# The last group of an MLP's second product, as seven half-size products instead of one plain product

## The chip, the cores and the metric

The kernel runs on one core of a Trainium2 chip. The core has five engines that run side by side and meet through semaphores: TensorE (PE, matmuls; its weight loads are the row PEld), VectorE (DVE), ScalarE (ACT), GpSimd (POOL) and SyncE (SP). Transfers between the chip's memory and the core's SBUF are issued here by SP and by GpSimd. The metric is the time of one execution on the device in microseconds (us); a smaller one is better.

## The reference

Two layers of a bidirectional encoder, 512 tokens by 1024 features, float32. Layer 0 mixes tokens with a gated delta rule (GDN), layer 1 with gated linear attention (GLA); after each mixer and after each MLP stands a layer norm of the scaled residual sum. The change lies in the MLP and the norms:

```
def _sq_relu_mlp(h, w1, w2):
    a = jax.nn.relu(jnp.matmul(h, w1))
    return jnp.matmul(a * a, w2)

for i in range(DEPTH):
    m = _mixer_gdn(...) if i % 2 == 0 else _mixer_gla(...)
    x = _layernorm(DEEPNORM_ALPHA * x + m, ln1_g[i], ln1_b[i])
    x = _layernorm(DEEPNORM_ALPHA * x + _sq_relu_mlp(x, mlp_w1[i], mlp_w2[i]), ln2_g[i], ln2_b[i])
```

`w1` is 1024 by 4096, `w2` 4096 by 1024.

## The kernel before

**Precision.** Each float32 operand of a matmul is split into two parts, `hi` and `lo` (`split`, L85): ScalarE casts the operand to `hi` (L95), VectorE subtracts `hi` from it (L96). `mm3` (L111) then issues three matmuls for one product of tiles: `hi*hi`, `hi*lo`, `lo*hi`. Tiles that hold parts are called `wh`/`wl`, `w2h`/`w2l`, `ah`/`al`, `xh`/`xl`; a tag with `bufs` buffers is a ring, so a new tile waits until the oldest one in it has been read for the last time.

**The MLP** works in four groups of 1024 of the 4096 features. The first product makes the activations `h` of a group, the second product multiplies them by 1024 rows of `w2` and adds to the residual `xt` (four tiles of 128 tokens, two halves of 512 columns each). Groups 0 to 2 of the second product run in `second` as seven products of half size: `h` is cut into quarters (`a11`, `a12`: tokens 0 to 255, features 0 to 511 and 512 to 1023; `a21`, `a22`: tokens 256 to 511), `w2` into blocks `(0,0)`, `(0,1)`, `(1,0)`, `(1,1)` of 512 by 512, and sums and differences of these are multiplied. A block is two tiles `w2r` (`q` = 0, 1) of 128 by 1024; `plus` adds one block to another in place on VectorE (L351). Each of the seven products is 24 matmuls of 512 columns, into two PSUM banks with the tags X, Y or Z, and `add` (L464) adds a bank to the residual. Between the products, `nxt` issues the pieces of the first product of the following group, so that VectorE and ScalarE have time for sums and parts.

**The last group** (`last`) has no following group. It computes the plain product: for each of the four token tiles and each column half, 8 x 3 matmuls of 512 columns (bank `pl`), 192 in all, a tile at a time; after each tile follow its two adds and its layer norm, and then either its four-by-two transposes into the next mixer's input (`xpose`, first MLP) or its store (second MLP). The weights are staged by `wrows` through the ring `wst` and split into whichever rings are free.

**The norm** (`layernorm`) has two forms. With `sums` the mean comes from accumulators of the adds and the squares from ScalarE; without, VectorE takes statistics (L223, L224). Then `(x - mean) * g` (L226), the reciprocal root on ScalarE and VectorE (L186 to L195), and `* rstd + b` (L231). Except for the last tile, the second column half of this final step is a ScalarE multiply (L233) and a GpSimd add (L234):

```
for q in range(2):
    if last or q == 0:
        nc.vector.scalar_tensor_tensor(out[q], out[q], rstd[:, 0:1], par[2 + q], ALU.mult, ALU.add)
    else:
        nc.scalar.mul(out[q], out[q], rstd[:, 0:1])
        nc.gpsimd.tensor_tensor(out[q], out[q], par[2 + q], ALU.add)
```

That form runs in the norms after the two mixers; `last` calls with `last=True`.

**Order.** Each engine works through its own list in order. A scheduler sets these lists from the program and from the dependences of the tiles; inside `in_order(engine)` the instructions of that engine keep the order in which they are written.

Of the kernel before, what the change touches and what calls it, by code (L numbers as in the profile page):

```python
# [17 lines left out]
P = 128  # L18
S = 512
# [9 lines left out]
class Ctx:  # L29
# [54 lines left out]

    def split(self, src, shape, pool=None):  # L85

        nc = self.nc
        if pool is None:
            hi = self.whl.tile(shape, F32R, name="wh", tag="wh")
            lo = self.whl.tile(shape, F32R, name="wl", tag="wl")  # L90
        else:
            pool, hi, lo, bufs = pool
            hi = pool.tile(shape, F32R, name=hi, tag=hi, bufs=bufs)
            lo = pool.tile(shape, F32R, name=lo, tag=lo, bufs=bufs)
        nc.scalar.copy(hi, src)  # L95
        nc.vector.tensor_tensor(lo, src, hi.bitcast(F32), ALU.subtract)  # L96
        return hi, lo
# [28 lines left out]

    def proj_halves(self, specs, between=None):


        out = [self.bank([P, S], F32, name=name, tag=tag) for _, name, tag in specs]  # L130
        for hf in range(2):
            sl = slice(hf * 256, hf * 256 + 256)
            for ps, ((wh, wl), _, _) in zip(out, specs):
                n = wh.shape[-1]
                for k in range(KT):
                    if wl is None:
# [70 lines left out]
    def layernorm(self, z, out, par, last=False, sums=None):  # L207
# [21 lines left out]
        for q in range(2):  # L229
            if last or q == 0:  # L230
                nc.vector.scalar_tensor_tensor(out[q], out[q], rstd[:, 0:1], par[2 + q], ALU.mult, ALU.add)  # L231
# [70 lines left out]
def mlp(c, w1, w2, g, b, out=None, extra=None):  # L302
# [14 lines left out]
    with c.banks(pj=2, X=2, Y=2, Z=2), tc.tile_pool(name="mlp", bufs=2) as pool:  # L317
# [20 lines left out]

        def split(i):

            i_, j_ = {1: (0, 0), 2: (1, 0), 3: (1, 1), 4: (1, 0), 5: (0, 0), 6: (0, 0), 7: (0, 1)}[i]
            parts[i] = [c.split(blocks[i_, j_, q], [P, 2, 512], pool=ring("w2")) for q in range(2)]

            sums = {1: ((0, 0), (0, 1)), 2: ((0, 1), (1, 1)), 5: ((0, 0), (1, 1)), 6: ((1, 0), (0, 0))}
            if i in sums:
                plus(*sums[i])

        def plus(a, b):
# [117 lines left out]
        def quarters(h):  # L466
            return [h[j][:, :, HT * i:HT * i + HT] for i in range(2) for j in range(2)]

        def second(gi, h, a, nxt):

            a11, a12, a21, a22 = quarters(h)

            def banks(tag):
                return [c.bank([P, 512], F32, name="p" + tag, tag=tag) for _ in range(2)]

            def product(bk, a, i, new, by_tile=False):

                if i not in parts:
                    split(i)
                ws = parts.pop(i)  # L480
                order = [(q, j) for j in range(2) for q in range(2)] if by_tile else [(q, j) for q in range(2) for j in range(2)]
                for q, j in order:
                    wh, wl = ws[q]
                    sl = slice(j * P, (j + 1) * P)
                    for k in (2 * q, 2 * q + 1):
                        c.mm3(bk[j], a[0][:, k, sl], a[1][:, k, sl], wh[:, k % 2, :], wl[:, k % 2, :],
                              new and k == 0, k == HF - 1, skip_group_check=True)

            def fetch(i, j):
                if gi + 2 < G:  # L490
                    load(gi + 1, i, j)

            X, Y = banks("X"), banks("Y")
            load(gi, 1, 0)
# [3 lines left out]
            nxt()  # L498
            Z = banks("Z")
            product(Z, pair(a12), 2, True)  # L500
# [27 lines left out]
            nxt()  # L528
            if gi + 2 == G:
                nxt()  # L530
                nxt()
# [6 lines left out]

        def last(gi, h):

            par = c.load_ln(g, b, lambda i: pool.tile([P, 512], F32, name="ln", tag=("xh5", "xh6", "xl5", "xl6")[i], bufs=1))
            a, ws = {}, {}

            def part(i, j, home):
                a[i, j] = pair(h[j][:, :, HT * i:HT * i + HT], home)

            def rows(i, home=None):
                ws[i] = c.wrows(w2, (gi * GF + 2 * (i % 4)) * P, i // 4 * 512, pool=ring(home) if home else None)

            rows(0)  # L550
            rows(3, "w2")
            part(0, 0, "ah")
            rows(1)
            rows(2)
            part(0, 1, "raw")
            rows(4, "raw")
            rows(5, "raw")
            rows(6, "w2")
            rows(7, "w2")
            part(1, 0, "ah")  # L560
            part(1, 1, "raw")
            if out is None:
                c.new_x()
            for t in range(NT):
                sl = slice(t % 2 * P, t % 2 * P + P)
                for hf in range(2):
                    ps = c.bank([P, 512], F32, name="pl", tag="YZYZXZXZ"[2 * t + hf])
                    for k in range(GF):
                        wh, wl = ws[4 * hf + k // 2]
                        ah, al = a[t // 2, k // HF]  # L570
                        c.mm3(ps, ah[:, k % HF, sl], al[:, k % HF, sl], wh[:, k % 2, :], wl[:, k % 2, :], k == 0, k == GF - 1)
                    add(t, hf, ps)
                c.layernorm(c.xh(t), c.xh(t), par, last=True)
                if out is None:
                    c.xpose(t, c.xt[t], ("pj",))
                else:
                    nc.sync.dma_start(out[t * P:(t + 1) * P, :], c.xt[t])

# [32 lines left out]
        for gi in range(G - 1):  # L611
            more = gi + 2 < G
            nh = new_h()

            def nxt():
# [16 lines left out]
                step += 1  # L632
                if half == 1 and i % 4 == 2 and more:
                    split(1)
# [50 lines left out]
def gla(c, gc, w_in, gate_w2, w_out, ln_g, ln_b, w_next):  # L685
# [5 lines left out]
    with c.banks(ac=2, tp=2, pj=4), tc.tile_pool(name="gla", bufs=2) as pool:  # L691
# [943 lines left out]
```

## Time and profile before

| | us |
|---|---|
| median of three runs | 1375.24 |
| the three runs | 1370.43, 1375.24, 1376.11 |
| the profiled execution | 1370.78 |
| its span, first to last instruction | 1369.1 |
| last group of the first MLP, first to last matmul `pl` | 721.81 to 770.3 |
| last group of the second MLP, first to last matmul `pl` | 1315.51 to 1360.4 |

The profile is of one execution. A row of the timeline reads: start, duration, engine, line, operation, output<-inputs, shape, count, and in brackets how long the engine idled before it and what ended that. A duration reaches from an instruction's start to its end; instructions of one engine overlap a little, so the time that one occupies is the distance to the next start. In a row of the waits stand the waiting instruction, what it waited for, the total, the number of waits and the longest. In the row of a window stand its length and the busy time of PE, PEld, DVE, ACT and POOL, each with its count, then the granted clock, the DMA share and GB/s. In the chain of waits, followed back from the last instruction, a row is start, length and who held the chain.

### The profile page before, as it was taken

Reading aid. Unit: us, or ns where it says so; the run is one execution under the profiler, and the core shown is the slowest. Engines: PE = TensorE matmul, PEld = TensorE weight load, DVE = VectorE, ACT = ScalarE, POOL = GpSimd, SP = SyncE. Lnnn points to the kernel's source line nnn. Section 1 sums busy time; section 2 is a strip of 40 time slices with the busy share of each in tenths; the row PEclk is TensorE's granted clock in tenths of the full one; section 3 lists DMA queues with packets and bytes.
Section 4 is the critical chain, followed back from the end, with each engine's and each line's share of the span. In section 5 each row is a group of like instructions: output and inputs, shape, how many; then the busy total and the mean of one; then the engine's idle time right before and its main releaser. Section 6 shows DMA issues by size and latency. Waiting matters only on the chain.

```text
span 1369.1 us, 21146 instructions
## 1 busy us (share of the span) xinstructions
PE 1341.5 (98%) x8317; PEld 1123.9 (82%) x8317; DVE 1073.9 (78%) x1685; ACT 738.7 (54%) x1444; POOL 72.5 (5%) x111
## 2 busy tenths in 40 slices
PE   8999999999999999999999999999999999999997
PEld 7777777777777888888887888888878888888886
DVE  7787787778677997897967687977779787979675
ACT  4776668765743655555553354654446455545440
POOL 5000000000003700000000000000000000000000
PEclk9999999999999999999999999999999999999999
DMA  6221112210251523243123332221325153322141
GB/s 190 63 62 48 47 32 63 60 35 32 78 154 57 176 78 108 77 154 93 47 90 100 91 92 76 62 62 62 99 55 185 47 154 92 124 78 60 47 152 49
DMA packets 145222, 117.44 MB, mean 86 GB/s; under 512 B 6571, under 2 KB 121379, under 8 KB 145123
## 3 DMA queue, kind: packets, MB, share of 16 engines
q1 hardware_dynamic: 143779, 111.90, 27.2%
q0 software_dynamic: 1344, 4.20, 1.1%
q8 instruction: 65, 1.06, 0.3%
q14 instruction: 34, 0.28, 0.1%
HBM read 113.99 MB, written 2.10 MB: 85 GB/s over the span
## 4 chain that ended last, share of the span: by engine, by line
PE 83%; ACT 7%; DVE 6%; DMA 2%; issue 1%; POOL 0%; DVEq 0%; SPq 0%; ACTq 0%
PE pj L115 5%; PE pj L116 5%; PE pj L114 5%; PE pX L114 3%; PE pX L115 3%; PE pX L116 3%; PE pjv L114 3%; PE pjv L115 3%; PE pjv L116 3%; PE fxz L114 2%; PE scp L865 2%; PE op L1561 2%; PE fxz L115 2%; PE fxz L116 2%; PE pl L115 2%; PE pl L116 2%
## 5 line engine op out<-in xcount | busy, mean ns | idle before, releaser
L95 ACT CAST wh<-wst 128x1024 fp32r<-128x1024 f32 x146 | 152.8, 1050 | 203.8 <-PE pj L115 49.8
L96 DVE TENSOR_TENSOR wl<-wst,wh 128x1024 fp32r<-128x1024 f32 x146 | 178.9, 1232 | 62.2 <-ACT wh L95 62.1
L115 PE MATMUL pj<-xtl,wh 128*128 128x512 f32 (+1 forms) x352 | 127.1, 361 | 0.5 <-DVE xtl L178 0.5
L114 PE MATMUL pj<-xth,wh 128*128 128x512 f32 (+1 forms) x352 | 126.8, 362 | 0.8 <-ACT xth L177 0.7
L116 PE MATMUL pj<-xth,wl 128*128 128x512 f32 (+1 forms) x352 | 126.7, 361 | 0.0
L96 DVE TENSOR_TENSOR w2l<-w2r,w2h 128x1024 fp32r<-128x1024 f32 x84 | 102.5, 1222 | 26.6 <-ACT w2h L95 26.5
L95 ACT CAST w2h<-w2r 128x1024 fp32r<-128x1024 f32 x84 | 88.2, 1050 | 64.5 <-PE pX L116 28.1
L114 PEld LDWEIGHTS pj<-xth,wh 128*128 128x128 f32 x352 | 66.2, 189 | 11.2 <-ACT xth L177 1.2
L115 PEld LDWEIGHTS pj<-xtl,wh 128*128 128x128 f32 x352 | 66.4, 189 | 10.9 <-DVE xtl L178 0.8
L115 PE MATMUL pX<-w2l,ah 128*128 128x512 f32 x192 | 75.0, 391 | 0.0
L116 PE MATMUL pX<-w2h,al 128*128 128x512 f32 x192 | 74.9, 390 | 0.0
L114 PE MATMUL pX<-w2h,ah 128*128 128x512 f32 x192 | 74.8, 393 | 0.0
L116 PEld LDWEIGHTS pj<-xth,wl 128*128 128x128 f32 x352 | 66.4, 189 | 10.2
L95 ACT CAST ah<-h 128x1024 fp32r<-128x1024 f32 x46 | 48.4, 1053 | 46.8 <-PE pX L115 20.8
L351 DVE TENSOR_TENSOR w2r<-w2r 128x1024 f32<-128x1024 f32 x48 | 58.1, 1233 | 0.3
L96 DVE TENSOR_TENSOR al<-h,ah 128x1024 fp32r<-128x1024 f32 x46 | 56.2, 1221 | 0.6
L114 PE MATMUL pjv<-wh,xth 128*128 128x512 f32 x128 | 54.7, 427 | 0.0
L116 PE MATMUL pjv<-wh,xtl 128*128 128x512 f32 x128 | 50.2, 392 | 0.0
L115 PE MATMUL pjv<-wl,xth 128*128 128x512 f32 x128 | 50.0, 390 | 0.0
L116 PEld LDWEIGHTS pX<-w2h,al 128*128 128x128 f32 x192 | 36.1, 188 | 7.5
L116 PE MATMUL pjk<-xth,wl 128*128 128x512 f32 (+1 forms) x112 | 41.8, 373 | 0.0
L114 PEld LDWEIGHTS pX<-w2h,ah 128*128 128x128 f32 x192 | 35.8, 188 | 7.1 <-ACT w2h L95 0.3
(469 smaller groups left out, 3915.4 us busy)
## 6 DMA issues: line engine op xcount, KB each, us to landing
wst<-in_mlp_w SPq DMA_DIRECT2D x80, 512.0 KB, 4.3
w2r<-in_mlp_w SPq DMA_DIRECT2D x48, 512.0 KB, 3.7
wst<-in_a_w_in SPq DMA_DIRECT2D x32, 512.0 KB, 4.1
wst<-in_b_w_in SPq DMA_DIRECT2D x32, 256.0 KB, 3.0
wst<-in_a_w_out SPq DMA_DIRECT2D x8, 512.0 KB, 3.8
wst<-in_b_w_in SPq DMA_DIRECT2D x8, 512.0 KB, 3.8
wst<-in_b_w_out SPq DMA_DIRECT2D x8, 512.0 KB, 3.6
xt<-in_x SPq DMA_DIRECT2D x4, 512.0 KB, 4.1
```

The source lines that it names most:

```text
L95: nc.scalar.copy(hi, src)
L96: nc.vector.tensor_tensor(lo, src, hi.bitcast(F32), ALU.subtract)
L114: mm(ps, ah, bh, start=start, stop=False, **kw)
L115: mm(ps, ah, bl, start=False, stop=False, **kw)
L116: mm(ps, al, bh, start=False, stop=stop, **kw)
L351: V.tensor_tensor(blocks[a + (q,)], blocks[a + (q,)], blocks[b + (q,)], ALU.add)
L865: T.matmul(ps[:, n, :], kh[:, sl], qh[:, sl], start=True, stop=True)
L1561: T.matmul(op[:, n, :], l, r, start=i == 0, stop=i == len(mm) - 1)
```

## The change

`last` becomes a form of `second` without a following group: seven products of 24 matmuls, 168 instead of 192, in the order 1, 5, 2, 6, 3, 7, 4, into banks X, Y, Z, X, Y, X, X. The products 3, 7 and 4 go tile by tile (`by_tile`), so that a token tile is complete before the product ends. Its blocks of `w2` are loaded ahead as in the other groups.

- The sums of blocks in the last group (`plus` with `by_dma`) are adding transfers that GpSimd issues, SBUF to SBUF, 512 KB each, eight in an MLP.
[...]
- The second part of a block gets homes that have fallen free: the operands' tiles `xh`/`xl`, a tile of `h`, a ring `wh`/`wl`.
- In the last group the lists of GpSimd, ScalarE and VectorE are written out by hand up to product 3, that of PE throughout.
- The accumulating form of `add` (`full`) gives the sums for the norm's first form; all four norms follow product 3. Tiles 0 and 1 are transposed inside product 4, tiles 2 and 3 inside the first projections of the mixer that follows (`at` in `proj_halves`). The output is stored in halves of a tile.
- The norm's final step is always VectorE's: no GpSimd add, no ScalarE multiply.

```diff
-    def split(self, src, shape, pool=None):
+    def split(self, src, shape, pool=None, by_dma=False):
...
         nc.scalar.copy(hi, src)
-        nc.vector.tensor_tensor(lo, src, hi.bitcast(F32), ALU.subtract)
+        if by_dma:
+            nc.scalar.mul(lo, src, -1.0)
+            nc.gpsimd.dma_start(lo, src, accum_op=ALU.add)
+        else:
+            nc.vector.tensor_tensor(lo, src, hi.bitcast(F32), ALU.subtract)
         return hi, lo
...
         for q in range(2):
-            if last or q == 0:
+            if True:
                 nc.vector.scalar_tensor_tensor(out[q], out[q], rstd[:, 0:1], par[2 + q], ALU.mult, ALU.add)
...
+            if homes:
+                for x, y in {1: (((0, 0), (0, 1)), ((0, 1), (1, 1))), 5: (((0, 0), (1, 1)),), 2: (((1, 0), (0, 0)),)}.get(i, ()):
+                    plus(x, y, True)
+                return
...
-                V.tensor_tensor(blocks[a + (q,)], blocks[a + (q,)], blocks[b + (q,)], ALU.add)
+                if by_dma:
+                    nc.gpsimd.dma_start(blocks[a + (q,)], blocks[b + (q,)], accum_op=ALU.add)
+                else:
+                    V.tensor_tensor(blocks[a + (q,)], blocks[a + (q,)], blocks[b + (q,)], ALU.add)
...
             if gi + 2 == G:
+                split(4)
                 nxt()
                 nxt()
...
+        def last(gi, h, a):
...
+            load(gi, 1, 0)
+            X, Y, Z = banks("X"), banks("Y"), banks("Z")
+            split(5, homes[5])
+            V.tensor_tensor(a21, a22, a21, ALU.subtract)
+            a5 = pair(a21)
+            product(X, a, 1, True)
+            a2 = pair(a12)
+            split(2, homes[2])
+            V.scalar_tensor_tensor(a11, a21, -1.0, a11, ALU.mult, ALU.subtract)
+            for j in range(2):
+                add(j, 0, X[j])
+            product(Y, a5, 5, True)
+            a6 = pair(a11)
+            split(6, homes[6])
+            V.scalar_tensor_tensor(a12, a12, -1.0, a11, ALU.mult, ALU.subtract)
+            V.scalar_tensor_tensor(a21, a11, -1.0, a22, ALU.mult, ALU.subtract)
+            for j in range(2):
+                add(2 + j, 1, Y[j], ALU.subtract)
+            product(Z, a2, 2, True)
+            split(7, homes[7])
+            a3 = pair(a12)
+            for j in range(2):
+                full(j, 0, Z[j])
+            split(3, homes[3])
+            product(X, a6, 6, False)
+            t = wide(F32R)
+            split(4, homes[4], (None, t[:, 0:2, :], t[:, 2:4, :], None))
+            a7 = pair(a21)
+            for j in range(2):
+                add(j, 1, X[j], ALU.subtract)
+            product(Y, a3, 3, False, True)
+            orders.close()
+            full(0, 1, Y[0], -1.0)
+            a4 = pair(a22)
+            full(1, 1, Y[1], -1.0)
+            product(X, a7, 7, False, True)
+            norm(0, False)
+            for j in range(2):
+                full(2 + j, 1, X[j], -1.0)
+            norm(1, False)
+            product(X, a4, 4, False, True, turn)
+            for j in range(2):
+                full(2 + j, 0, X[j])
+            return norm
...
-            h, a = nh, nxt.a if more else None
-        last(G - 1, h)
+            h, a = nh, nxt.a
+        with c.in_order(mybir.EngineType.PE):
+            norm = last(G - 1, h, a)
+        norm(2, False)
+        norm(3, True)
...
-        gps, *qk0 = c.proj_halves(specs)
+        with c.in_order(mybir.EngineType.PE):
+            gps, *qk0 = c.proj_halves(specs, at={(0, 2, 4 * j): lambda t=2 + j: c.xpose(t, c.xt[t], ("tp", "pj")) for j in range(2)})
```

How the change moves instructions, at three places. In the rows the line numbers are those of the changed file (L101 is the subtraction of `split`, L479 is `add`, L579 is `full`, L181 a transpose); `xt_5637` to `xt_5640` are the residual tiles 0 to 3.

VectorE in the second MLP's last group, between products 1 and 3:

```order
L101 TENSOR_TENSOR al<-h,ah 128x1024 x2
L101 TENSOR_TENSOR w2l<-w2r,w2h 128x1024
L101 TENSOR_TENSOR xl_13604<-w2r,xh_13603 128x1024
L605 SCALAR_TENSOR_TENSOR h<-h 128x4x256
L479 TENSOR_TENSOR xt_5637<-xt_5637,pX 128x512
L479 TENSOR_TENSOR xt_5638<-xt_5638,pX 128x512
L101 TENSOR_TENSOR al<-h,ah 128x1024
L101 TENSOR_TENSOR w2l<-w2r,w2h 128x1024
L101 TENSOR_TENSOR xl_13645<-w2r,xh_13644 128x1024
L611 SCALAR_TENSOR_TENSOR h<-h 128x4x256
L612 SCALAR_TENSOR_TENSOR h<-h 128x4x256
L479 TENSOR_TENSOR xt_5639<-xt_5639,pY 128x512
```

These are the low parts of the left operands of products 5 and 2, the weights of 2, a difference of quarters, the adds of product 1, and the same again for product 6. Behind them come the second add of product 5, the low part of product 3's left operand, two `full` of product 2, and the low parts of product 3's weights. Before, the last group had only casts, subtractions and `pl` adds without sums of quarters.

VectorE at the end of the second MLP, before:

```order
L464 TENSOR_TENSOR xt_5640<-xt_5640,pl 128x512
L223 BN_STATS bst<-xt_5640 128x6
L224 BN_AGGR bmv<-bst 128x2
L226 SCALAR_TENSOR_TENSOR xt_5640<-xt_5640,bmv,ln 128x512
L188 TENSOR_TENSOR rst<-rsy 128x1
L226 SCALAR_TENSOR_TENSOR xt_5640<-xt_5640,bmv,ln 128x512
L189 SCALAR_TENSOR_TENSOR rst<-bmv,rst 128x1
L190 TENSOR_SCALAR rst<-rst 128x1
L195 TENSOR_TENSOR rstd<-rsy,rst 128x1
L231 SCALAR_TENSOR_TENSOR xt_5640<-xt_5640,rstd,ln 128x512 x2
```

and with the change:

```order
L238 SCALAR_TENSOR_TENSOR xt_5637<-xt_5637,rstd,ln 128x512 x2
L197 TENSOR_SCALAR rst<-rst 128x1
L579 SCALAR_TENSOR_TENSOR xt_5639,lns<-pX,xt_5639 128x512
L202 TENSOR_TENSOR rstd<-rsy,rst 128x1
L224 SCALAR_TENSOR_TENSOR bmv<-lns,bias_83 128x1
L238 SCALAR_TENSOR_TENSOR xt_5638<-xt_5638,rstd,ln 128x512 x2
L579 SCALAR_TENSOR_TENSOR xt_5640,lns<-pX,xt_5640 128x512
L227 SCALAR_TENSOR_TENSOR bmv<-lnq,bias_81 128x1
L233 SCALAR_TENSOR_TENSOR xt_5639<-xt_5639,bmv,ln 128x512
```

The last add of tile 3 (`xt_5640`, L579) now stands behind the ends of the norms of tiles 0 and 1, and what is left of the norm of tile 2 stands between it and the norm of tile 3.

PE at the end of the first MLP, before and with the change:

```order
L116 MATMUL pl<-w2h,w2r 128x512
L174 MATMUL tp<-ident,xt_5639 128x128 x8
L114 MATMUL pl<-w2h,w2r 128x512
L115 MATMUL pl<-w2l,w2r 128x512
L116 MATMUL pl<-w2h,w2r 128x512
```

```order
L121 MATMUL pX<-xh_8568,al 128x512
L181 MATMUL tp<-ident,xt_5637 128x128 x8
L119 MATMUL pX<-h,ah 128x512
L120 MATMUL pX<-h,ah 128x512
L121 MATMUL pX<-h,al 128x512
L119 MATMUL pX<-h,ah 128x512
L120 MATMUL pX<-h,ah 128x512
L121 MATMUL pX<-h,al 128x512
L181 MATMUL tp<-ident,xt_5638 128x128 x8
L119 MATMUL pX<-xh_8568,ah 128x512
```

Before, a tile's transposes stood some 20 matmuls behind its last one; now those of tile 0 stand right behind the first half of product 4, 36 matmuls (product 7's 24 and 12 of product 4) behind the end of product 3, the last product that writes tiles 0 and 1, and those of tile 1 six matmuls later.

More of the change, by code (lines that the diff above doesn't have):

```diff
@@ L498, in second @@
             nxt()
-            Z = banks("Z")
+            Z = banks(tags[1])
             product(Z, pair(a12), 2, True)
@@ L537, in second @@
                 nxt()
[L539 to L561, printed above, removed]
+        def last(gi, h, a):
+            homes = {i: (pool, f"xh{k}", f"xl{k}", 1) for i, k in ((5, 3), (2, 7), (6, 6), (7, 3), (4, 7))}
+            homes[3] = ring("raw")
+            wide = lambda dt: pool.tile([P, HF, S], dt, name="h", tag="h", bufs=3)
+            a11, a12, a21, a22 = quarters(h)
+            sums = [c.small.tile([P, 2], F32, name="lns", tag="lns") for t in range(NT)]
+            par = []
+            for src, tag in ((g, "xh5"), (b, "xl5")):
+                t = pool.tile([P, 2, 512], F32, name="ln", tag=tag, bufs=1)
+                nc.gpsimd.dma_start(t, src.rearrange("(q n) -> q n", q=2).partition_broadcast(P))
+                par += [t[:, 0, :], t[:, 1, :]]
@@ L562, in last @@
             if out is None:
                 c.new_x()
[L564 to L573, printed above, removed]
-                if out is None:
-                    c.xpose(t, c.xt[t], ("pj",))
-                else:
-                    nc.sync.dma_start(out[t * P:(t + 1) * P, :], c.xt[t])
+            ET = mybir.EngineType
```

78 lines of the change are left out of this document (51 added, 27 removed).

## The prediction

> **What bounds the kernel now.** I read the page, then PE's waits, the stages by windows, and last the timelines around the two places where the last group of an MLP runs.
>
> ```profile
> span 1369.1 us, 21146 instructions
> PE 1341.5 (98%) x8317; PEld 1123.9 (82%) x8317; DVE 1073.9 (78%) x1685; ACT 738.7 (54%) x1444; POOL 72.5 (5%) x111
> ...
> PE 83%; ACT 7%; DVE 6%; DMA 2%; issue 1%; POOL 0%; DVEq 0%; SPq 0%; ACTq 0%
> ```
>
> ```profile
> PE tp L174 <- POOL xt L234: 1.4, 3, 0.6
> PE pl L115 <- DVE w2l L96: 1.3, 2, 0.6
> PE pjq L114 <- DVE xt L464: 0.9, 1, 0.9
> ```
>
> PE is busy 98% of the span and its listed waits are small (total, times, longest), so a matmul less is worth its slot. That holds while the other engines keep up; for that I look at VectorE (DVE) by stage: the two norms after the mixers, and the last group of the second MLP (busy us of PE, PEld, DVE, ACT, POOL in turn).
>
> ```profile
> 415.00:440.00 25.00, 22.79 (x127) 17.64 (x127) 23.58 (x52) 9.11 (x20) 7.30 (x8) 1.00 0.00 1
> 1008.00:1036.00 28.00, 24.94 (x149) 20.45 (x149) 24.45 (x58) 12.89 (x30) 4.69 (x3) 1.00 0.03 8
> ...
> 1315.00:1361.00 46.00, 44.81 (x195) 36.02 (x194) 31.02 (x52) 9.62 (x16) 0.00 (x0) 1.00 0.18 68
> ```
>
> VectorE fills 94% and 87% of the norm stages but 67% of the last group. The change adds VectorE work to all three.
>
> **Durations.** Slots are differences of starts in these rows.
>
> ```profile
> 721.81 0.40 PE L114 MATMUL pl<-wh,ah 128*128 128x512 f32 x1
> ...
> 1290.16 0.39 PE L114 MATMUL pY<-w2h,ah 128*128 128x512 f32 x1
> 1290.84 0.39 PE L114 MATMUL pY<-w2h,ah 128*128 128x512 f32 x1
> ...
> 1311.05 0.28 PE L114 MATMUL fxz<-xth,wh 128*128 128x256 f32 x1
> 1311.41 0.40 PE L114 MATMUL pX<-w2h,ah 128*128 128x512 f32 x1
> 1315.51 0.39 PE L114 MATMUL pl<-wh,ah 128*128 128x512 f32 x1
> ...
> 762.84 1.29 PE L174 MATMUL tp<-ident,xt 128*128 128x128 f32 x8
> 763.89 0.48 PE L114 MATMUL pl<-w2h,w2r 128*128 128x512 f32 x1
> 787.58 0.63 PE L779 MATMUL lg<-glr,w2r 96*128 96x512 f32 x2
> ```
>
> Three 512-column matmuls take 0.68 us, so one 0.227 and a half-size product (24) 5.44; three of 256 columns 0.36; eight transposes 1.05. The last group starts at T = 721.81 and T = 1315.51.
>
> ```profile
> 1317.30 1.04 ACT L95 CAST w2r<-wst 128x1024 fp32r<-128x1024 f32 x1
> 1318.25 1.04 ACT L95 CAST ah<-h 128x1024 fp32r<-128x1024 f32 x1
> 1320.30 1.22 DVE L96 TENSOR_TENSOR al<-h,ah 128x1024 fp32r<-128x1024 f32 x1
> 1321.44 1.22 DVE L96 TENSOR_TENSOR w2r<-wst,w2r 128x1024 fp32r<-128x1024 f32 x1
> 1293.95 1.28 DVE L464 TENSOR_TENSOR xt<-xt,pY 128x512 f32<-128x512 f32 x2
> 1009.29 0.68 DVE L292 SCALAR_TENSOR_TENSOR xt<-ob,xt 128x512 f32<-128x512 f32 x1
> 1009.90 0.08 DVE L292 DVE_READ_ACCUMULATOR xt<-ob,xt 128x1 f32 x1
> 1364.13 1.41 DVE L231 SCALAR_TENSOR_TENSOR xt<-xt,rstd,ln 128x512 f32<-128x512 f32 x2
> ```
>
> So a cast costs ScalarE 0.95 (ready after 1.05), a 1024-wide subtraction or sum costs VectorE 1.14 (ready after 1.22), an add from PSUM 0.62, with its accumulator 0.70, a 512-wide norm step 0.67, a 128x1 step 0.1 to 0.2.
>
> **The matmuls.** Each MLP loses 24 of 192: 24 x 0.227 = 5.44, both 10.9. The two waits on w2l (0.6 each) belong to the removed loop. This is the ceiling; three things take from it.
>
> **Inside the last group (second MLP).** In VectorE's order, from the low part of the second product's left operand (its cast needs the first product's slot, free at T+5.6) to the low part of product 3's first weight, stand ten 1024-wide steps, four adds and two accumulating adds: 10 x 1.14 + 4 x 0.62 + 2 x 0.70 = 15.3, from T+6.7 to T+22, ready at T+23.2. Product 3 is the fifth; its second matmul is due at T + 4 x 5.44 + 0.23 = T+22.0. PE waits 1.3. Products 5, 2 and 6 just fit: for 5, sum, cast and low part end 0.3 before its third matmul wants them. ScalarE has 22 casts and multiplies there, 21 us of 38, and its slots never come last: covered. The low parts of products 7 and 4 leave VectorE (4 x 1.14 less) for ScalarE and the adding transfers, and so do eight block sums; I cost both at nothing, and they are hidden behind two to three products each, until a transfer is late (rival C). So five products end at T+28.5, all seven at T+39.4 (1354.9), against the last matmul's end now:
>
> ```profile
> 1360.20 0.24 PE pl L116
> ...
> 1360.46 0.70 DVE xt L464
> ...
> 1364.88 0.66 DVEq L1631
> ```
>
> **The tail (second MLP).** What is late next is VectorE. Before, tiles were finished one by one, with a norm some 11 us apart, and 5.1 us of VectorE followed the last matmul, to 1365.54. Now all four norms stand behind product 3: from the last operand's low part (T+28.5 + 1.05 cast + 1.22 and handovers = T+31.1) VectorE has four accumulating adds (2.8), sixteen norm steps (10.7), two statistics with their merge (1.6) and some 22 small steps (about 3.3): 18.4, done at T+49.5 = 1365.0. PE's 5.4 shrinks to 0.5. The last store is 256 KB instead of 512:
>
> ```profile
> wst<-in_b_w_in SPq DMA_DIRECT2D x32, 256.0 KB, 3.0
> ...
> wst<-in_b_w_in SPq DMA_DIRECT2D x8, 512.0 KB, 3.8
> ```
>
> by these loads 0.8 less. Together **-1.3**; bounds +1 (each handover 0.05 dearer) and -6 (no queue on VectorE).
>
> **The end of the first MLP.** Same walk: norm 0 ends at T+38.1 (no statistics there). Its transposes stand after the first half of product 4, T+36.7: PE waits 1.4. Those of tile 1 need norm 1, which stands behind tile 0's first low part: 0.95 more. Tile 2's need norm 2, 12.5 after norm 0, while PE has 10.5 of work: 1.95. Tile 3 fits. PE's work from T to the end of the projections of q and k is 168 x 0.227 + 4 x 1.05 + 128 x 0.117 = 57.3 (before 62.8 of the 65.8 measured from 721.81 to 787.58); with 1.3 + 1.4 + 0.95 + 1.95 it takes 62.9. **-2.8**; bounds -8.4 (no wait) and +2.8 (each wait twice).
>
> **Norms after the mixers.** GpSimd's adds go; VectorE gets six steps of 0.67 (4.0) and ScalarE loses six. Back come the 1.4 that transposes waited for POOL (row above), and this:
>
> ```profile
> 423.81 1.71 POOL L234 TENSOR_TENSOR xt<-xt,lnp 128x512 f32<-128x512 f32 x1 [27.80 <-ACT xt L233]
> 424.28 1.26 DVE L189 SCALAR_TENSOR_TENSOR rst<-bmv,rst 128x1 f32<-128x1 f32 x1
> ...
> 1009.90 0.15 DVE L189 SCALAR_TENSOR_TENSOR rst<-bmv,rst 128x1 f32<-128x1 f32 x1
> ...
> 1028.08 1.25 DVE L189 SCALAR_TENSOR_TENSOR rst<-bmv,rst 128x1 f32<-128x1 f32 x1
> ```
>
> a 0.15 us step lasts 1.26 under a GpSimd add, in each stage once: 1.1 each. First stage, where VectorE is the limit: +2.0 - 1.1 = +0.9. Second stage, where all three POOL waits lie: -1.4, and on the last tile's chain -1.1 + 0.67 = -0.4: -1.8. **-0.9**; bounds -3.6 (the steps hidden, all returned) and +4.0 (nothing returned). The Trainium skill, SBUF — State Buffer, "Who interferes with whom", states that a VectorE instruction with two SBUF inputs is blocked by a GpSimd instruction that reads SBUF; the trace agrees at the two rows above. By that rule alone other steps under the six adds could have been held too; the term would then go to its lower bound and the sum below to -7.7.
>
> **The adding transfers.** No row shows one. In each MLP there are eight sums of weight blocks and four low parts, 512 KB each. Nearest rows: 3.7 for a load of that size, and GpSimd's broadcasts:
>
> ```profile
> w2r<-in_mlp_w SPq DMA_DIRECT2D x48, 512.0 KB, 3.7
> ...
> DMA to landing us min/median/max: 3.8/6.2/7.4
> ```
>
> I bound one, issue to landing, by 3.7 and by twice 7.4 (two reads, one write), and take 7. The slack: the first that matters leaves after the split of block 1's second half, whose slot comes free with the pair's product 2 (now such a cast stands at 1302.63, its low part ends 1304.94 = T-10.6), and VectorE wants the sum split by T-0.2 on ScalarE: 10.4. The second hop (issued T+2.05, wanted T+13.3) has 11, the third about 10, low parts 12. At 7 they cost nothing. The row of that cast:
>
> ```profile
> 1302.63 1.05 ACT L95 CAST wh<-wst 128x1024 fp32r<-128x1024 f32 x1 [0.77 <-PE fxz L115]
> ```
>
> By the Trainium skill, DMA: Bandwidth & Descriptors, "Anatomy of one DMA", such a transfer would take an estimated 2.0 + 0.524/0.436 = 3.2 us; no run here shows it for an adding one. By it rival C would fall away and the sum would stay.
>
> **The rest.** The eight weight loads of the last group stay, earlier on SP's queue and into the ring of blocks; the output leaves in eight stores instead of four; the exchange of banks X and Z, the earlier split of block 4 and the transposes set among the gate's and q's matmuls in the mixer add no instruction. Nothing.
>
> **Sum.** -1.3 - 2.8 - 0.9 = -5.0, less than half of the 10.9. The profiled execution took 1370.78 (the span and 1.7 around it): 1365.8. It was near the fastest: the three runs are 1370.43, 1375.24 and 1376.11, and from their median the sum gives 1370.2. I say 1367, between the two and nearer the first because rival B pulls there.
>
> **Rivals.** B, *the late loads go*: the chain of waits holds 7.28 and 3.50 us of weight loads just before and in the last group, and PE waits at its end:
>
> ```profile
> 1306.43 7.28 DMA wst<-in_mlp_w
> ...
> 1320.41 3.50 DMA wst<-in_mlp_w
> ```
>
> If the 4.5 between the median and the profiled run is such a load coming later still, the change, which loads these blocks earlier, takes it off too: 1375.24 - 5.0 - 4.5 = 1365.7, which is 9.5 faster. Where VectorE's queue is also shorter than I walked, 10.9 and the two waits of 0.6 go: 1358.7. Against it: one profile cannot show that the spread lies there. C, *the adding transfers land late*: the place is ScalarE's queue in the last group. A cast that waits for a summed block holds every cast behind it, VectorE waits for the cast and PE for the low part. It starts from 10 us a transfer, and between 11 and 12 the gain is gone. At 14 the first hop makes product 5 late by 3.3, the second adds 3.1, the third 4.3: 10.7 an MLP, 21.4 - 5.0 = +16.4: 1387. For it: three hops in series, and GpSimd's queue is in order, with the two loads of norm parameters, which wait for a slot of the first product, ahead of the first hop. Against: every landing above is below 7.5. D, *VectorE eats it all*: no term of the MLPs is left, because each handover on VectorE costs a little more than the rows allow: 1370.78 - 0.9 = 1369.9 on the profiled run, no change.
>
> **How the numbers follow.** A measurement of this kernel tells about 0.5% (6.9 us) from no change. My forecast (with D) 0.48: its own range is 1360 to 1372, and a quarter of it lies beyond -6.9. B 0.32, all faster. C 0.20, all slower. Faster 0.12 + 0.32 = 0.44, same 0.36, slower 0.20. The range runs from B's 1358 to just below C's 1387.
>
> **What would show it.** Right: seven products with one wait of about 1.3 before the fifth; transposes of tile 0 waiting about 1.4 on VectorE; VectorE without a gap after the last matmul until about 10 us later; adding transfers landing in 4 to 9 us; no POOL wait of transposes. Wrong: waits of PE or ScalarE on GpSimd's queue (C); a VectorE tail of 5 us, or before runs whose last group waits longer (B).

## The result, and the profile after

The changed kernel takes 1363.07 us (median of 4 runs, 1359.91 to 1363.59), the kernel before 1375.46 (1370.43 to 1376.11): a ratio of 0.9913, 95% interval 0.9885 to 0.9941, so 12.4 us or 0.9% faster. The forecast was 1367, 8.2 below the median known then.

The profiled execution took 1362.81. Its page, first and fourth part:

```profile
span 1361.1 us, 21212 instructions
PE 1332.9 (98%) x8269; PEld 1118.8 (82%) x8269; DVE 1091.1 (80%) x1730; ACT 768.9 (56%) x1492; POOL 82.0 (6%) x125
...
PE 83%; DVE 7%; ACT 7%; issue 2%; DMA 0%; DVEq 0%; POOL 0%; SPq 0%; ACTq 0%; POOLq 0%
```

PE has 8.6 us less busy time, VectorE 17 more and ScalarE 30 more; in the chain that ended last VectorE has 7% instead of 6, and the DMA's 2% are gone. Where the time went is read from when the same matmul starts in both traces. These rows (start, duration in us) are of the changed kernel: the last group of the first MLP, the matmul behind the projections of q and k, and the last group of the second MLP.

```profile
724.11 0.39 PE L119 MATMUL pX<-w2h,ah 128*128 128x512 f32 x1
...
784.42 0.63 PE L845 MATMUL lg<-glr,w2r 96*128 96x512 f32 x2
...
1309.99 0.39 PE L119 MATMUL pX<-w2h,ah 128*128 128x512 f32 x1
```

Before, these three stood at 721.81, 787.58 and 1315.51. So the end of the first MLP, from the first row to the second, lasts 60.31 instead of 65.77. The second norm stage lies between these rows, of before and of the changed kernel (the last output transposes of the second mixer, and the first product of the next group):

```profile
1001.29 0.96 PE L972 MATMUL otp<-ident,o 128*128 128x128 f32 x7
...
1073.13 0.39 PE L114 MATMUL pX<-w2h,ah 128*128 128x512 f32 x1
```

```profile
998.31 0.96 PE L1038 MATMUL otp<-ident,o 128*128 128x128 f32 x7
...
1067.60 0.39 PE L119 MATMUL pX<-w2h,ah 128*128 128x512 f32 x1
```

The first norm stage is cut in the same way, from the last output transpose of the first mixer to the first product of the next group (414.71 to 478.91 before, 418.03 to 481.30 with the change). All stages, for the kernels that follow too (us; the bodies of the MLPs, 242.2 to 243.0, and the second mixer, 213.7 to 214.8, are left out):

| kernel | start to norm stage 1 | norm stage 1 | end of MLP 1 | norm stage 2 | end of MLP 2 |
|---|---|---|---|---|---|
| before | 414.7 | 64.20 | 65.77 | 71.84 | 53.59 |
| changed | 418.0 | 63.27 | 60.31 | 69.29 | 51.11 |
| e1 norms only | 415.2 | 63.25 | 65.28 | 69.22 | 53.62 |
| e2 group only | 414.6 | 64.19 | 60.28 | 73.37 | 51.35 |
| e3 no adding transfers | 416.8 | 63.27 | 69.18 | 69.21 | 58.82 |
| e4 before again | 419.9 | 64.21 | 64.80 | 71.86 | 53.88 |
| e5 idle GpSimd adds | 417.7 | 64.24 | 60.27 | 72.87 | 51.36 |
| e6 sums late, one copy | 417.8 | 63.26 | 61.34 | 69.18 | 51.10 |
| e7 sums late, two copies | 418.8 | 63.27 | 69.27 | 69.25 | 58.68 |
| e8 tail, tiles 0 and 1 | 416.0 | 63.26 | 60.25 | 69.34 | 51.74 |
| e9 product 3 too | 417.7 | 63.27 | 62.74 | 69.19 | 53.61 |
| e10 tail, tile 0 | 418.9 | 63.27 | 60.26 | 69.31 | 50.52 |

The four stages that the change touches give 0.93 + 5.46 + 2.55 + 2.48 = 11.4. The profiled runs differ by only 7.97, because the first 415 us, which the change does not touch, took 3.3 longer in the changed kernel's run (why, e4 shows).

### The profile page after: what moved, and what is told of

Its sections match the earlier page's. It is cut to its first block, busy times and chain, and to the rows that moved or that the text cites. A ratio compares the mean times of both kernels' runs of the same rounds, so it can differ in the third digit from the quotient of the medians.

```text
span 1361.1 us, 21212 instructions
## 1 busy us (share of the span) xinstructions
PE 1332.9 (98%) x8269; PEld 1118.8 (82%) x8269; DVE 1091.1 (80%) x1730; ACT 768.9 (56%) x1492; POOL 82.0 (6%) x125
## 4 chain that ended last, share of the span: by engine, by line
PE 83%; DVE 7%; ACT 7%; issue 2%; DMA 0%; DVEq 0%; POOL 0%; SPq 0%; ACTq 0%; POOLq 0%
PE pj L121 5%; PE pj L119 5%; PE pj L120 5%; PE pjv L119 3%; PE pX L119 3%; PE pX L120 3%; PE pjv L120 3%; PE pX L121 3%; PE pjv L121 3%; PE fxz L119 2%; PE fxz L120 2%; PE fxz L121 2%; PE scp L931 2%; PE op L1627 2%; PE pY L120 2%; PE pY L121 2%
## 5 line engine op out<-in xcount | busy, mean ns | idle before, releaser
L101 DVE TENSOR_TENSOR wl<-wst,wh 128x1024 fp32r<-128x1024 f32 x140 | 171.5, 1233 | 51.0 <-ACT wh L96 50.8
L101 DVE TENSOR_TENSOR w2l<-w2r,w2h 128x1024 fp32r<-128x1024 f32 x94 | 114.8, 1224 | 29.0 <-ACT w2h L96 29.0
L96 ACT CAST w2h<-w2r 128x1024 fp32r<-128x1024 f32 x96 | 100.7, 1049 | 63.9 <-PE pX L121 27.3
L96 ACT CAST ah<-h 128x1024 fp32r<-128x1024 f32 x56 | 58.9, 1052 | 66.2 <-PE pY L120 22.5
L101 DVE TENSOR_TENSOR al<-h,ah 128x1024 fp32r<-128x1024 f32 x56 | 68.4, 1222 | 6.8 <-ACT ah L96 6.1
L120 PE MATMUL pX<-w2l,ah 128*128 128x512 f32 x168 | 65.6, 390 | 0.0
L121 PE MATMUL pX<-w2h,al 128*128 128x512 f32 x168 | 65.5, 390 | 0.0
L119 PE MATMUL pX<-w2h,ah 128*128 128x512 f32 x168 | 65.3, 393 | 0.0
L364 POOL DMA_DIRECT2D w2r<-w2r x16 | 13.8, 863 | 616.5 <-DVE w2l L101 594.8
L120 PE MATMUL pY<-w2l,ah 128*128 128x512 f32 x112 | 43.9, 392 | 1.3 <-DVE w2l L101 1.3
L121 PE MATMUL pY<-w2h,al 128*128 128x512 f32 x112 | 43.8, 391 | 0.0
```

Of the source, the lines that this page charges most:

```text
L119: mm(ps, ah, bh, start=start, stop=False, **kw)
L120: mm(ps, ah, bl, start=False, stop=False, **kw)
L121: mm(ps, al, bh, start=False, stop=stop, **kw)
L364: nc.gpsimd.dma_start(blocks[a + (q,)], blocks[b + (q,)], accum_op=ALU.add)
```

## The experiments

**e1, e2: the two parts alone.** e1 is the kernel before with this edit:

```diff
-            if last or q == 0:
+            if True:
                 nc.vector.scalar_tensor_tensor(out[q], out[q], rstd[:, 0:1], par[2 + q], ALU.mult, ALU.add)
```

e2 is the changed kernel with that line as before, and `True` for `last` in the norms of the last groups.

> The kernel before with one edit: the norms after the mixers multiply by rstd and add ln_b on VectorE alone (no ScalarE multiply, no GpSimd add); the last groups stay as they were. Theory A (from the two traces set side by side): the norms are worth 3.5 us, 0.9 in the first stage and 2.6 in the second, so 1371.9 from a median of 1375.4. Theory B (the prediction's terms): 0.9 in all, the first stage 0.9 dearer and the second 1.8 cheaper, so 1374.5; the other 2.6 that the traces show belong to the changed group. Told apart by the step in the start times of the same matmuls across the two norm stages.

> The changed kernel with the norms after the mixers as before (ScalarE multiply and GpSimd add in three of the four tiles); the last groups are the changed ones. Theory A: the two parts add up; the group is worth 5.5 in the first MLP and 2.5 in the second, so 8.0 faster than before, 1367.4, and the stages of the norms stand as in the kernel before. Theory B: the group gives 10.5 of the 11.3 and the norms 0.9: 1364.9.

e1: 1369.92 against 1374.98 of the kernel before on the same chip, ratio 0.9962 (0.9947 to 0.9977, which is 3.2 to 7.3 us); the table has 0.95 and 2.62 less in the norm stages: theory A. e2: 1367.15, ratio 0.9943 (0.9929 to 0.9956); its MLP ends lose 5.49 and 2.24. The parts add up: by the stages 3.6 and 7.7, which is 11.3 of the 11.4. One thing was not expected: norm stage 2 of e2 is 1.5 longer than before. The view by windows shows why (the PE clock is the third number from the end):

```profile
1025.00:1030.00 5.00, 3.53 (x22) 2.69 (x21) 5.00 (x8) 2.52 (x4) 0.00 (x0) 0.91 0.07 15
1030.00:1035.00 5.00, 5.00 (x34) 5.00 (x33) 4.96 (x5) 0.00 (x0) 0.00 (x0) 0.74 1.05 343
```

The granted clock was 0.91 and 0.74 in these windows; 5 x 0.09 and 5 x 0.26 make an estimated 1.7, enough for the 1.5. The waits of PE in front of it (0.41, 0.43, 0.84 and 0.55) are those of the kernel before and of e4, whose clock stayed at 1.00 there, so they do not account for the dip, and whether the edit has a part in it is not shown.

**e4: where the spread of the kernel before lies.**

> The kernel before, unchanged, for another profile. Theory A: runs of one kernel differ by dips of the granted clock in the first 55 us: a run near 1375 shows stretches below 0.8 there and the same matmuls 3 to 6 us later from there on, with the last groups as in the profile of before; a run near 1370 shows no dip. Theory B (the prediction's rival of late loads): a run near 1375 has the clock at 1.00 throughout, and PE waits for a weight load in or before a last group.

1375.42. The windows 10 to 15 and 40 to 45 us in the first profile of before, of the changed kernel, and of e4:

```profile
10.00:15.00 5.00, 5.00 (x46) 5.00 (x45) 3.13 (x5) 2.63 (x6) 0.00 (x0) 1.00 0.81 214
40.00:45.00 5.00, 5.00 (x27) 3.94 (x26) 3.66 (x5) 4.61 (x12) 0.00 (x0) 1.00 0.21 49
```

```profile
10.00:15.00 5.00, 5.00 (x33) 5.00 (x33) 1.57 (x3) 1.60 (x4) 0.00 (x0) 0.70 0.89 236
40.00:45.00 5.00, 5.00 (x19) 3.97 (x19) 2.56 (x9) 2.15 (x5) 0.00 (x0) 0.66 0.29 85
```

```profile
10.00:15.00 5.00, 5.00 (x37) 5.00 (x36) 2.06 (x4) 1.90 (x4) 0.00 (x0) 0.77 0.72 200
40.00:45.00 5.00, 5.00 (x15) 3.93 (x15) 2.37 (x8) 1.37 (x4) 0.00 (x0) 0.50 0.32 94
```

PE is busy throughout in all three and does 73, 52 and 52 matmuls there. e4 is 5.2 late when it reaches norm stage 1; its last groups take 64.80 and 53.88, together 0.7 less than in the first profile, and PE waits for no transfer in either. Theory A: these two runs differ by dips of the granted clock in the first 50 us, not by late weight loads. Other runs of the kernel before have no trace, but a mean clock: 26 of them lie between 1371.6 (clock 0.997) and 1378.5 (0.993), and 0.004 of 1375 is 5.5 of these 6.9 us. Where in those runs the clock fell is not known. The 0.97 by which the end of the first MLP differs between the two profiles, with the clock at 1.00 in both, stays open.

**e5: what the norms gained from.** Behind each of the six norms that had a GpSimd add before:

```diff
                 nc.vector.scalar_tensor_tensor(out[q], out[q], rstd[:, 0:1], par[2 + q], ALU.mult, ALU.add)
+                if q and not last and not sums_mlp:
+                    spare = self.small.tile([P, 512], F32, name="spare", tag="spare", bufs=1)
+                    nc.gpsimd.tensor_tensor(spare, out[q], par[2 + q], ALU.add)
```

> The changed kernel with one GpSimd addition more behind each of the six norms that had one before; it reads the finished half tile and ln_b and writes a spare tile that nobody reads. Theory A (the gain of the norms came from GpSimd no longer standing in the way of VectorE): VectorE steps of 0.15 us last 1.2 again, and 1.1 or more of the 3.5 us comes back in each stage. Theory B (the gain came from the shorter chain, nobody waits for GpSimd's result any more): no more than 0.3 us per stage comes back. Read from the start times of the same matmuls across the norm stages.

1367.43. Norm stage 1 takes 64.24, all of the 0.97 back. In stage 2 the clock dipped (0.50 from 1030 to 1035), behind a wait of PE that is 1.75 here and 0.77 in the changed kernel; up to the last tile's transposes, which start before the dip, the same matmuls stand 1.0 later than in the changed kernel (1028.34 against 1026.55, of which 0.76 is the offset of the run). The rows of stage 2, first GpSimd, then VectorE:

```profile
1025.61 1.28 POOL L241 TENSOR_TENSOR spare<-xt,ln 128x512 f32<-128x512 f32 x1 [8.06 <-DVE rst L196]
```

```profile
1025.76 1.14 DVE L202 TENSOR_TENSOR rstd<-rsy,rst 128x1 f32<-128x1 f32 x1
```

A product of two 128x1 tiles, 0.16 us elsewhere, ends with the GpSimd add that nobody waits for. In each stage one of the three adds meets such a step (1.16 us in stage 1): theory A, at 1.0 per stage, a little less than the 1.1 that it asked for. The Trainium skill, SBUF — State Buffer, "Who interferes with whom", says that a VectorE instruction with two SBUF inputs contends with a GpSimd instruction that reads SBUF. The trace agrees at both places, and the steps of VectorE that read PSUM ran under the adds at their usual 0.69.

**e3: without the adding transfers.**

```diff
-                    plus(x, y, True)
+                    plus(x, y, False)
...
-            parts[i] = [c.split(blocks[i_, j_, q], [P, 2, 512], homes if homes and q else first or ring("w2"), bool(homes) and i in (7, 4))
+            parts[i] = [c.split(blocks[i_, j_, q], [P, 2, 512], homes if homes and q else first or ring("w2"), False)
```

> The changed kernel with the eight sums of weight blocks and the four low parts of each MLP's last group on VectorE instead of ScalarE and the adding transfers. Theory A (VectorE sets product 3 and all behind it): VectorE gets 12 x 1.14 = 13.7 us more per MLP; PE waits some 8 to 10 us in front of products 5 to 3, and the second MLP ends 10 to 13.7 later: 20 to 27 slower than the changed kernel, 1383 to 1390. Theory B (VectorE has room in the group before, where its order may take the first sums): half of that, 1373 to 1377.

1378.63, ratio to before 1.0029 (1.0018 to 1.0039): 15.6 slower than the changed kernel. The ends of the MLPs are 8.9 and 7.7 longer, less than theory A's 10 to 13.7, more than theory B's half. PE's waits (total, times, longest):

```profile
PE pY L120 <- DVE w2l L101: 7.3, 2, 4.3
PE pY L119 <- ACT ah L96: 3.5, 2, 2.1
```

So the place is theory A's (product 5's operand and product 3's low part). The waits are not all of the loss. The clock, 1.00 at these places in the changed kernel, falls behind them; the rows are of the first MLP and of the second:

```profile
755.00:760.00 5.00, 5.00 (x16) 4.00 (x15) 4.16 (x7) 0.69 (x2) 0.00 (x0) 0.63 0.00 0
1350.00:1355.00 5.00, 5.00 (x18) 3.98 (x18) 3.57 (x7) 0.81 (x2) 0.00 (x0) 0.74 0.00 0
```

Taken over whole dips this is up to 5.1 in the first MLP and 3.4 in the second (an estimate, clock missing times length; the part that falls into a wait costs nothing). PE's waits in front of these products come to 12.0 with the 1.2 on product 5's low part, 10.7 above the changed kernel's 1.3, which is some 5.4 an MLP. So more than half of VectorE's 13.7 must have found idle time. Without the adding transfers, and with their work on VectorE as here, the seven products are slower than the eight: the ends of the MLPs take 128.0 together, 119.4 before, and up to 8.5 of the difference is the clock's.

**e6, e7: when the adding transfers come late.** In front of each block sum one copy (e6) or two (e7):

```diff
                 if by_dma:
+                    nc.gpsimd.dma_start(wait, blocks[a + (q,)][:, 0, 0:128])
                     nc.gpsimd.dma_start(blocks[a + (q,)], blocks[b + (q,)], accum_op=ALU.add)
```

> The changed kernel with one small copy (64 KB of the same block to a spare tile) in front of each of the eight block sums, so that each adding transfer waits for a landing first: 3 to 4 us for the first half of a pair, twice that for the second. Theory A (the prediction's: nothing is lost up to some 10 us from issue to landing, since the sums have that much slack): at most 1 us per MLP. Theory B (the sums are on the path already): 3 us or more per MLP.

> The same with two small copies in a row in front of each sum: 6 to 8 us for the first half of a pair, 12 to 16 for the second, so 12 to 20 from the time the sum could start to its landing. Theory A (rival C's price): past 10 to 12 us product 5 and those behind it are late, 6 to 11 us per MLP, 12 to 22 slower than the changed kernel, with ScalarE's casts waiting for transfers. Theory B (the slack is wider than walked): under 3 per MLP.

1363.81 and 1380.04. e6 loses 1.0 in the first MLP and nothing in the second; e7 loses 9.0 and 7.6. Theory A in both, though not at product 5: products 5, 2 and 6 were not late in either MLP. PE's two longest waits in e7, one in each MLP:

```profile
PE pX L119 <- DVE xt L482: 5.8, 1, 5.8
PE pY L120 <- DVE w2r L101: 5.3, 2, 4.7
```

They have different causes. In the first MLP it is the one that the prediction's rival C names, at the last sum instead of the first. ScalarE's cast of the second part of product 4's block waits for that sum, the casts of left operands stand behind it, and VectorE and the bank X wait for those:

```profile
755.67 1.04 ACT L96 CAST xh<-w2r 128x1024 fp32r<-128x1024 f32 x1 [4.73 <-DMA w2r<-w2r]
758.64 1.23 DVE L101 TENSOR_TENSOR al<-h,ah 128x1024 fp32r<-128x1024 f32 x1 [8.03 <-ACT ah L96]
```

In the second MLP VectorE stood still at another step:

```profile
1347.55 1.23 DVE L101 TENSOR_TENSOR w2r<-w2r 128x1024 fp32r<-128x1024 f32 x1 [5.10 <-issue]
```

`w2r` is here the second low part of product 3's weights. Its home is a slot of the ring of blocks, and the slot's block is still being read by the last of the third pair of sums, issued at 1342.77. So a late sum can hold up a cast or a slot. In the changed kernel these rows bound the slot, the issue of that sum and the step that needs the slot:

```profile
1320.33 0.85 POOL L364 DMA_DIRECT2D w2r<-w2r  x1 [0.28 <-DVE xl L101]
```

```profile
1332.75 1.22 DVE L101 TENSOR_TENSOR w2r<-w2r 128x1024 fp32r<-128x1024 f32 x1
```

That is 12.4 from issue to need; for the cast in the first MLP it is 12.2 (734.68 to 746.89). Here, too, part of the loss is the clock, which fell during both waits:

```profile
760.00:765.00 5.00, 4.39 (x12) 3.56 (x13) 3.68 (x9) 1.42 (x4) 0.00 (x0) 0.59 1.05 207
1350.00:1355.00 5.00, 5.00 (x14) 3.88 (x13) 3.03 (x5) 0.48 (x1) 0.69 (x1) 0.54 1.05 198
```

These windows alone make an estimated 2.1 at most of the 9.0 and 2.3 of the 7.6.

**e8, e10: less VectorE work in the tail.** In the norms of tiles 0 and 1 (e10: tile 0) of the second MLP:

```diff
-                nc.vector.scalar_tensor_tensor(out[q], out[q], rstd[:, 0:1], par[2 + q], ALU.mult, ALU.add)
+                nc.scalar.mul(out[q], out[q], rstd[:, 0:1])
+                nc.gpsimd.dma_start(out[q], par[2 + q], accum_op=ALU.add)
```

> The changed kernel; in the second MLP the last step of the norms of tiles 0 and 1 (times rstd, plus ln_b) is a ScalarE multiply and an adding transfer of ln_b instead of a VectorE step: four steps of 0.67 leave VectorE. Theory A (VectorE alone sets the end behind the last matmul): the end comes 2.4 to 2.7 earlier, 1360.5 against the changed kernel's 1363.1. Theory B (the other engines are as full there): the multiplies delay the squares of tile 2 or the transfers and stores of tile 1 land last, between 0.5 earlier and 1 later.

> The changed kernel with the ScalarE multiply and adding transfer of ln_b for tile 0 of the second MLP alone (e8 did it for tiles 0 and 1). Theory A (in e8 the four multiplies held up tile 2's squares on ScalarE, and tile 1's stores, late behind its transfers, held up tile 3's on SyncE's queue; VectorE's two steps do count): the span from the last group's start to the end is 1.0 to 1.4 shorter than the changed kernel's 51.1. Theory B (behind the last matmul only tile 3's own chain counts): within 0.3 of it.

e8: 1362.42, ratio to before 0.9910 (0.9895 to 0.9926), no different from the changed kernel; its end of MLP 2 is 0.6 longer. e10: 0.6 shorter, between the theories. The add of tile 3's last half and the last norm step, in the changed kernel, in e8 and in e10:

```profile
1349.94 0.69 DVE L579 SCALAR_TENSOR_TENSOR xt<-pX,xt 128x512 f32<-128x512 f32 x1
...
1356.44 1.41 DVE L238 SCALAR_TENSOR_TENSOR xt<-xt,rstd,ln 128x512 f32<-128x512 f32 x2
```

```profile
1348.12 0.69 DVE L579 SCALAR_TENSOR_TENSOR xt<-pX,xt 128x512 f32<-128x512 f32 x1 [1.69 <-PE pX L121]
...
1354.62 1.42 DVE L238 SCALAR_TENSOR_TENSOR xt<-xt,rstd,ln 128x512 f32<-128x512 f32 x2
```

```profile
1350.29 0.69 DVE L579 SCALAR_TENSOR_TENSOR xt<-pX,xt 128x512 f32<-128x512 f32 x1 [0.49 <-PE pX L121]
...
1356.79 1.41 DVE L238 SCALAR_TENSOR_TENSOR xt<-xt,rstd,ln 128x512 f32<-128x512 f32 x2
```

In each the second of these starts 6.5 behind the first. Relieved, VectorE waits 1.69 or 0.49 for the last matmul, and what follows it is as long as ever. In e8 the stores come later besides: SyncE's queue, which is in order, stood for tile 1's adding transfers, and the end came 4.5 behind VectorE's last step instead of 3.3. e10's 0.6 is far below what the runs can tell, so no version here is shown to be faster than the changed kernel.

**e9: product 3's low parts by adding transfers too** (`i in (7, 4, 3)`, and its split ahead of product 7's).

> The changed kernel; the two low parts of product 3's weights, too, are made by ScalarE and adding transfers instead of VectorE, and its split stands ahead of that of product 7 in the program. Theory A (PE's wait in front of product 3 is VectorE's queue, which is 2.3 us shorter then): the waits of 0.6 and 0.7 on w2l go, 0.7 to 0.9 us per MLP, and the second MLP's tail starts as much earlier: 1.4 to 1.8 in all. Theory B (the ring slots that product 3's parts need come free only when the third pair of block sums lands, and ScalarE's queue stands still for it): product 3 or 7 waits for a transfer, 1 to 5 us slower per MLP. Read from the start times of the same matmuls.

1367.27; 2.4 and 2.5 longer at the ends of the MLPs. Slower as theory B had it, for another reason:

```profile
1334.72 0.50 PE L119 MATMUL pY<-w2h,ah 128*128 128x512 f32 x1 [0.88 <-ACT ah L96]
```

ScalarE waited for no transfer there; it worked without a gap from 1323 to 1333. The cast of product 3's left operand stood behind the four casts and four multiplies of products 3 and 7, where in the changed kernel it stands behind the two and two of product 7 alone, and came 3.8 later after the group's start (T + 21.7 instead of T + 18.0). Of the four steps more, two are the new multiplies and two the casts of product 3, which the edit's order put ahead. Which of the two cost the time was not tried apart; with the splits in the old order the result could be another.

## Why the prediction was right, point by point

The time, 1363.07, lies 3.9 from the forecast and on its side of before. The sum behind it does not come as close: it had -5.0, less than half of the 11.4 by which the stages fell, and each of its three terms was too small. That the forecast was near is in part luck, as the paragraph on the rivals says.

**The bound and the order of events** held: four products end and product 3, the fifth, waits for a low part on VectorE, the last matmul ends at T + 39.3 (1309.99 to 1349.29; predicted 39.4), then VectorE works until T + 47.9 (predicted 49.5). PE's waits:

```profile
PE pY L120 <- DVE w2l L101: 1.3, 2, 0.7
PE tp L181 <- DVE xtl L185: 1.2, 3, 0.8
PE tp L181 <- DVE xt L238: 1.0, 1, 1.0
```

The list still has 1.3 for product 3, in both MLPs together; by the starts of the matmuls the product takes 6.3 and 6.4 instead of 5.44, so 0.9 and 1.0 are lost, predicted 1.3 each. No transposes wait for GpSimd.

**The second MLP:** -2.5 instead of -1.3. VectorE's last low part came 0.6 earlier than walked, and its work behind it was 17.3 instead of 18.4, the small steps being the cheaper part:

```profile
1339.31 1.22 DVE L101 TENSOR_TENSOR al<-h,ah 128x1024 fp32r<-128x1024 f32 x1
```

The 17.3 runs from this row's end at T + 30.5 to the end of the last norm step at T + 47.9. The smaller stores gave 0.3 behind VectorE's end (3.56 to 3.25), not 0.8.

**The end of the first MLP:** -5.5 instead of -2.8, and this is the largest miss; it was a size, not a mechanism. VectorE's norm steps and PE's matmuls and transposes around tile 0 and tile 1:

```profile
760.05 1.41 DVE L238 SCALAR_TENSOR_TENSOR xt<-xt,rstd,ln 128x512 f32<-128x512 f32 x2
762.77 1.41 DVE L238 SCALAR_TENSOR_TENSOR xt<-xt,rstd,ln 128x512 f32<-128x512 f32 x2
```

```profile
760.86 1.31 PE L181 MATMUL tp<-ident,xt 128*128 128x128 f32 x8
...
763.57 1.32 PE L181 MATMUL tp<-ident,xt 128*128 128x128 f32 x8
...
772.04 1.23 PE L181 MATMUL tp<-ident,xt 128*128 128x128 f32 x8 [1.05 <-DVE xt L238]
```

Two things were overlooked or too dear. The transposes of a tile's first half need only the first half of its norm: PE starts them at 760.86, when the second half is still being made. I made them wait for the whole norm. And the norm itself ended at T + 37.3, not 38.1. So the waits predicted as 1.4, 0.95 and 1.95 were 0.2, 0.2 and 1.2 by the starts of the matmuls, and with product 3's 0.9 they are 2.5 instead of 5.6. Of the 3.1 that this gives, 0.5 is lost again, half of it in products 1 and 5, which took 5.52 and 5.61 instead of 5.44. Put otherwise: beyond PE's work as the prediction adds it up, 62.8 before and 57.3 now, the stage takes 3.0 before and 3.0 now, so the whole saving of 24 matmuls arrives. Two profiles of before and e1 spread over 64.8 to 65.8 there, so the gain itself is 4.5 to 5.5.

**The norms:** -3.5 instead of -0.9. Of the term's pieces, GpSimd's hold on VectorE (1.1 a stage; e5: 1.0) and the 1.4 of waits on GpSimd were right. What failed was the price of the added VectorE steps, 0.67 each: three in the first stage (2.0) and one in the second (0.67). Without these 2.7 the term is -3.6, its lower bound for steps that are hidden, and e1 alone measures -3.6. In stage 1 e5 has the added steps with GpSimd's hold back in place and takes 64.24, as long as before (64.20): there the steps cost nothing on balance. Whether the shorter way from a norm to its transposes pays for a part of them, no run separates. VectorE's share of 94% of that stretch was read as "the limit". But the last transposes of stage 1 moved back, as VectorE had it, while PE did not wait longer. Before, and changed:

```profile
442.15 0.66 PE L174 MATMUL tp<-ident,xt 128*128 128x128 f32 x4
```

```profile
447.23 0.66 PE L181 MATMUL tp<-ident,xt 128*128 128x128 f32 x4
```

That is 1.8 later once the 3.3 of the run's start is taken off; PE did projections on the tiles that were ready in the meantime, and its waits in the stage fell from 2.2 to 1.1. So VectorE, though nearly full, was not the limit here, since PE had other work.

**The adding transfers:** assumed 7 us, slack about 10, costing nothing. Measured, for the sixteen block sums (issues, then issue to landing; within the 4 to 9 us that the prediction named):

```profile
L364 POOL DMA_DIRECT2D w2r<-w2r x16: 842/851/969, 696.4 to 1320.3; - x16
...
DMA to landing us min/median/max: 4.4/5.5/7.9
```

The Trainium skill, DMA: Bandwidth & Descriptors, "Anatomy of one DMA", led to an estimate of 3.2; the measurement decides. By e6 and e7 rival C's point of 10 to 12 us was about right (12.2 and 12.4). Its price was too high: it put 10.7 an MLP on 14 us, while in e7 the last sum was through 20.1 and 17.6 behind the changed kernel's issue (both counted from the group's start) and the loss was 9.0 and 7.6, a part of it the clock's. Its mechanism, a cast that holds the casts behind it, appeared in the first MLP of e7, at the last sum and not the first.

**The rivals.** B, late loads, had 0.32 of the chance; e4, a run near the median, shows dips of the clock in its place. It pulled the forecast from 1370.2, where the sum from the median lay, to 1367; the pull went the right way for a reason that wasn't there, which is luck. Rightly summed, the four stages give 11.4 off the median of before, 1364.1, within the spread of the 1363.07 measured. C and D did not happen.

## What to carry to other kernels

Cost added work on a busy engine at its full duration only after finding who waits for it and whether that engine has other work at hand; three steps on an engine 94% busy were free in one stage here. Follow a handover at the grain at which it happens: half a tile was enough for the next engine. And compare two traces stage by stage, from one matmul to the same matmul, before believing a difference of two totals: here 3.3 us of the difference lay where nothing had been changed.

## What the runs showed of the hardware

The granted TensorE clock fell in some executions and stayed at 1.00 at the same place in others of the same kernel (the windows of before and of e4 above). In the twelve traces, up to the last matmul, there are 21 such dips. Each holds the clock at 0.50, for 3.4 or 6.8 us, and so takes up to 1.7 or 3.4. The changed kernel's profile has two short ones in its first 50 us and starts its first norm stage 3.3 later than before; e4 has a short and a long one and is 5.2 late.

In 20 of the 21 the dip begins 1.7 to 3.5 us after PE has begun a wait of 1.2 to 5.8 us (in e7 at 757.2, in a wait that began at 754.8); e2's follows two shorter waits, 0.84 and 0.55. Waits alone do not decide it: the first profile of before has waits of 2.0 and 1.3 in its first 50 us and no dip. What does was not tried. For the reader this means that a wait can cost more than its length, as in e3 and e7.

An adding transfer of 512 KB within SBUF lands after 4.4 to 7.9 us and keeps GpSimd busy for 0.85 while it is issued. When several stood close together in e7, those of the low parts took 6.8 to 10.9 in the median.
